# The second mixer's modulation blocks moved behind its projections, eight loads to a PSUM bank, and the output weights' low parts on VectorE

## The chip, the cores and the metric

The kernel runs on one core of a Trainium2 chip, in one launch. The metric is device time in microseconds (us): 2055.61 us, the median of 3 runs of the kernel before (2055.24 to 2056.08). About 4 us (0.2%) is what a comparison of this kernel can tell from no change.

## The reference, cut to what matters

Two transformer layers on 512 latent and 256 context tokens of width 1024. Both layers are scaled and shifted by rows that come out of a conditioning vector; layer 1 (odd) has differential attention, and each layer ends in a mixture of 32 experts.

```python
mod = jax.nn.silu(c) @ w_mod[l] + b_mod[l]          # (6 * 1024) values: six rows
sh1, sc1, gt1, sh2, sc2, gt2 = jnp.split(mod[:, None, :], 6, axis=-1)
h_lat = modulate(x, norm_mix[l], sh1, sc1)          # before the mixer
o_lat, o_ctx = mixer_c(h_lat, h_ctx, ...)           # projections, attention, @ w_out
x = x + gt1 * o_lat                                 # row 2
tokens = modulate(x, norm_ffn[l], sh2, sc2)         # rows 3 and 4
f = hier_moe(tokens, w_group[l], ...)               # router, then experts
x = x + gt2 * f                                     # row 5
```

The row products for layer 1 are a matrix of 1024 x 6144; rows 0 and 1 are made in the first mixer. Rows 2 to 5 (two blocks of 2048 columns, each in 8 loads of 128 x 2048 floats, 1 MB) are made in the second mixer, and they are what moves here.

## The kernel before, in words

Layer 1 runs in four stages, one after another: the second mixer (`mixer_c`), the output projection with the router (`out_proj`), the sorting of tokens by expert, and the experts (`moe`), whose weights stream from HBM.

**The mixer.** It works in 8 groups (heads). A group's projection (L261 to L263, three float32r products per piece, into the one bank of pool `ctp`, tag "pp") gives q, k and v for 6 token tiles; then 4 units, one per 128 latent tokens, make scores (L596 to L604), a maximum on VectorE (L1914), two exponentials on ScalarE (L1918), a combination on VectorE (L1931), transposes on TensorE (L618), their copies (L622) and the product with v (L633). The projection of group g+1 is laid among the units of group g; the last group's four units come after all projections.

**The order.** `Sched` is a list planner: each piece has an engine, an assumed duration, what it depends on, which buffers it takes and gives, and a position `pos`; among ready pieces of an engine, the lowest `pos` goes first. That fixes the program order of TensorE (PE), VectorE (DVE), ScalarE (ACT) and GpSimd (POOL), each of which runs strictly in its order. SyncE (SP) issues nearly all DMAs; its order follows from the rest, and it too goes in order: a DMA whose buffer is not free holds up all behind it.

**The modulation blocks.** `mod_later` loads a block's 8 tiles (L376) into the ring of four 1 MB buffers `wr`, which the projections' weights (L1738), the output weights (L1047) and the first expert weights (L1249) use as well. Each tile is multiplied by the silu columns (L381: 4 products of 128x512 in float32, which the trace shows as 8 records). Two tiles are summed in one bank of the pool that the transposes use (tag "pt", two banks), then added to a row buffer in `oo` by DVE (L475). After the 8 tiles the row goes to `modrow` in DRAM (L497); the second block is first multiplied with the norm's gain (L491). `first` and `end` spread the tiles over positions CM0 to CM1; CMW is how many tiles may be loaded ahead.

**The output weights.** `prepare_out` loads 4 MB of `w_out_c` and splits each half tile into a float32r high part on ACT (L322) and a low part (L325), the latter on POOL in layer 1. It begins when the projections and the rotary embedding (POOL, L550 to L566) are done, since its tiles take their memory; so do the router's weights (L1030 to L1033).

**`out_proj`.** Per token tile: transposes (L1105), their high and low parts (L1112, L1119), 48 products (`pop`, L261 to L263), the gate row `bc2` (L1159), the residual (L1162) and the router's logits (L1217). `fold_router` folds rows 3 and 4 into the router's weights: it loads them from `modrow` as columns (L1264, tile `mrows`, in two DMAs), transposes them on PE (L1269) and goes on with L1272, L1276 and L1281. Row 4 is in the second block. L503 spreads rows over 128 partitions, L1093 loads the residual.

```python
ld = S.op("DMA", 2.95, lambda k=k, load=load: load(k), [mms[-LA]], take=("wr", "mw"))
a = S.op("DMA", 0.6, load, pos=-9.0)                      # fold_router: mrows <- modrow
a = S.op("PE", 0.11, flip, [a], take=("pl",), pos=1.0)    # L1269
```

Of the kernel before, what the change touches and what calls it, by code (L numbers as in the profile page):

```python
# [20 lines left out]
KD = 8  # L21
# [59 lines left out]
CPREP = 3.79  # L81
CPACK = 0.8
CP0 = -37.415
CMW = 1
CM0 = 1.0
CM1 = 28.601
DPE = .217
DDVE = 0.15
DACT = .119
# [146 lines left out]
class Backbone:  # L236
# [197 lines left out]
        return self.mod_columns(0, lambda: st["row"], [a], psp, tag)  # L434


    def mod_later(self, jobs, rows_tile, nf, silp, psp, tag, first, end, after):
        nc, S = self.nc, self.S
        total, n, out = KD * len(jobs), 0, {}
        ready = S.op("POOL", 0.5, lambda: self.mod_sil(silp), [after], pos=first)  # L440
        mms = [ready] * LA
        for l, g in jobs:
            st = {}

            def rows(l=l, g=g, st=st):
                st["row"] = rows_tile()
                if (l, g) == (1, 0):
                    return
                nc.gpsimd.memset(st["row"], 0.0)
                if g == 2:  # L450
                    nc.gpsimd.memset(nf, 0.0)

            def biases(l=l, g=g, st=st):
                if (l, g) == (1, 0):
                    return
                for j in range(4):
                    b = 512 * (4 * g + j)
                    nc.sync.dma_start(st["row"][32 * j:32 * j + 2], self.i["b_mod"][l, b:b + 512].partition_broadcast(2))
                    if g == 2 and j < 2:
                        nc.sync.dma_start(nf[32 * j:32 * j + 2], self.i["norm_ffn"][l, 512 * j:512 * j + 512].partition_broadcast(2))  # L460

            def load(k, l=l, g=g, st=st):
                st[k] = self.mod_load(l, g, k)

            def mm(k, st=st):
                if k % 2 == 0:
                    st["ps"] = psp.tile([128, 512], F32, tag=tag, name="pmod")
                self.mod_mm(st["ps"], silp, st[k], k, k % 2 == 0, k % 2 == 1)

            def add(k, l=l, g=g, st=st):  # L470
                r = st["row"]
                if k == 1 and (l, g) == (1, 0):
                    nc.vector.tensor_copy(r, st["ps"])
                else:
                    nc.vector.tensor_tensor(r, st["ps"], r, op=OP.add)  # L475

            S.pos = first + (end - first) * n / total
            a = S.op("POOL", 0.4, rows, [ready], take=("mrow",))
            a = S.op("DMA", 0.3, biases, [a])
            for k in range(KD):  # L480
                S.pos = first + (end - first) * n / total
                n += 1
                ld = S.op("DMA", 2.95, lambda k=k, load=load: load(k), [mms[-LA]], take=("wr", "mw"))
                mms.append(S.op("PE", 1.0, lambda k=k, mm=mm: mm(k), [ld, mms[-1]], take=() if k % 2 else ("pt",), give=("wr", "mw")))
                if k % 2:
                    a = S.op("DVE", 0.62, lambda k=k, add=add: add(k), [mms[-1], a], give=("pt",))
            if (l, g) == (1, 0):
                out[l, g] = self.mod_columns(l, lambda st=st: st["row"], [a], psp, tag, ("mrow",))
                continue
            if g == 2:  # L490
                a = S.op("DVE", 0.62, lambda st=st: nc.vector.scalar_tensor_tensor(  # L491
                    st["row"][0:64], st["row"][0:64], 1.0, nf[0:64], op0=OP.add, op1=OP.mult), [a])

            def store(l=l, g=g, st=st):
                for j in range(4):
                    b = 512 * (4 * g + j)
                    nc.sync.dma_start(self.modrow[l][:, b:b + 512], st["row"][32 * j:32 * j + 2])  # L497

            out[l, g] = S.op("DMA", 0.3, store, [a], give=("mrow",))
        return out  # L500
# [510 lines left out]
    def prepare_out(self, l, wout, pos, after):  # L1011

        nc, S, i = self.nc, self.S, self.i
        self.pre, self.wo, parts = ExitStack(), [], {}
        pool = lambda n, b, **k: self.pre.enter_context(self.tc.tile_pool(name=n, bufs=b, **k))
        self.pool_out = ExitStack()

        def room():
            rp = pool("route", 1)
            t = lambda n, sh, d=F32: rp.tile(sh, d, name="r" + n)  # L1020
            self.rt = {
                "idx": t("idx", [128, NST], I32), "sw": t("sw", [128, 2, NST]), "ps": t("ps", [CAP, 2, NE]),
                "ord": t("ord", [1, NE], I32), "idx2": t("idx2", [128, NE], I32), "sw2": t("sw2", [128, 2, NE]),
                "idxb": t("idxb", [CAP, 8], I32), "swb": t("swb", [CAP, 2, 8]), "base": t("base", [128, NE]), "nb": t("nb", [NE, 2]), "ad": t("ad", [128, 2 * NT], I32),
                "pay": t("pay", [128, NT, 2, 2]), "tb": t("tb", [1, 3 * NOVB], I32), "oh": t("oh", [128, NT, 2, NE]),
                "w": t("w", [128, NT, 2]), "cum": t("cum", [128, NT + 1, NE]), "rank": t("rank", [128, NT, 2]),
                "ids": t("ids", [128, NT]), "wrt": t("wrt", [128, KD, 36]), "brt": t("brt", [128, 36]),
            }
            wrt, brt = self.rt["wrt"], self.rt["brt"]
            nc.sync.dma_start(wrt[:, :, 0:4], i["w_group"][l].rearrange("(k p) n -> p k n", k=KD))  # L1030
            nc.sync.dma_start(wrt[:, :, 4:36], i["w_expert"][l].rearrange("(k p) n -> p k n", k=KD))
            nc.sync.dma_start(brt[:, 0:4], i["b_group"][l].partition_broadcast(128))
            nc.sync.dma_start(brt[:, 4:36], i["b_expert"][l].partition_broadcast(128))  # L1033
            self.stay = pool("wmoe", NMOE)
            rest = self.pool_out.enter_context(self.tc.tile_pool(name="opw", bufs=KD - NMOE))
            for k in range(KD):
                w = (self.stay if k < NMOE else rest).tile([128, 2, 1024], F32R, tag="wr", name="wo")
                self.wo.append((w[:, 0], w[:, 1]))

        S.pos = pos  # L1040
        start = S.op("-", 0.0, room, after)
        for q in range(4):
            S.pos = pos + 2 * q

            def load(q=q):
                w = parts[q] = self.wtile().rearrange("p (k f) -> p k f", k=2)
                nc.sync.dma_start(w, wout[q * 256:(q + 1) * 256].rearrange("(k p) f -> p k f", p=128))  # L1047

            ld = S.op("DMA", 2.95, load, [start], take=("wr",))
            for k in range(2):  # L1050
                self.split_ops(lambda q=q, k=k: (*self.wo[2 * q + k], parts[q][:, k]), 1024, [ld], give=("wr",) if k else (),
                               low_on="POOL" if l else "DVE")


    def out_proj(self, l, oo, first, gain=None):
# [746 lines left out]
    def mixer_c(self, oo):  # L1802
        nc, tc, i = self.nc, self.tc, self.i
        S = self.S = Sched((DPE, DDVE, DACT, DPOOL), (EPE, EDVE, EACT, EPOOL), wr=NW, pt=2, s=2, po=1, pp=1, p0=2, p1=2, pts=2, qdup=1, qhl=2, rt=1, rt1=1, hss=2, khl=1,
                           grp=2, vv=3, whl=5, mrow=2, mw=CMW)
        keep, st = ExitStack(), ExitStack()
# [3 lines left out]
        pss, psm = right("cts", 2, space=PSUM), right("ctm", 2, space=PSUM)  # L1810
        pso, psp = right("cto", 1, space=PSUM), right("ctp", 1, space=PSUM)
# [23 lines left out]
        ld = S.op("DMA", 8.0, lambda: None)  # L1835

        sd = [S.op("DMA", 1.5, lambda t=t: nc.sync.dma_start(oo[:, t], self.source(1, t)), [ld]) for t in range(NT)]
        ld = S.op("DMA", 1.0, loads, sd)
# [7 lines left out]
        hdone, spare = {}, []  # L1846
# [23 lines left out]
        a = S.op("POOL", 0.5, lam_dots, [ld], pos=-20.0)  # L1870
        a = S.op("DVE", 0.2, lambda: nc.vector.tensor_reduce(ls, lp[:, 0::2], axis=AX.X, op=OP.add), [a], pos=-20.0)
        a = S.op("ACT", 0.1, lambda: nc.scalar.activation(ls, ls, AF.Exp), [a], pos=-20.0)
# [4 lines left out]
        end = self.in_proj(0, c, CP0, 0.0, [tables])  # L1877
        c.hdone = lambda t, q: []
        ropes = end
        for g in range(7):  # L1880
# [6 lines left out]
        room = [oo[:, 4 + m // 2, 512 * (m % 2):512 * (m % 2) + 512] for m in range(4)]  # L1887
        rows = iter(room[0:2])
        self.mod_later([(1, 1), (1, 2)], lambda: next(rows), room[2], room[3][:, 0:256].rearrange("p (k f) -> p k f", k=KD),
                       psm, "pt", CM0, CM1, S.op("-", 0.0, lambda: None, spare))  # L1890
        prev = dict.fromkeys(("s", "t", "v"))
        packed, squares = {}, {t: [] for t in range(4)}
        for j, (g, t) in enumerate(units):
# [163 lines left out]
```

## Time and profile before

| what | value |
|---|---|
| median of 3 runs | 2055.61 us |
| the profiled execution | 2057.26 us, its span 2055.5 us |
| PE busy | 1803.5 us (88%) |
| DVE, ACT, POOL busy | 984.2, 547.7, 316.7 us |
| DMA | 533.11 MB, 259 GB/s over the span |
| the second mixer, about | 1042 to 1456 us |
| `out_proj` of layer 1, about | 1456 to 1511 us |

How to read it: times are from the span's start. The stage in question lies between two stretches in which the DMA engines are full (the experts of layer 0 until about 1020 us, those of layer 1 from about 1533 us). In the mixer itself the DMA engines carry little, and PE is the busy one until the last projection; after it comes a stretch of some 50 us in which no engine is full. "Idle before" in a row is the time that the engine stood still before it, with the engine that released it.

### The profile page before, as it was taken

What the parts mean: (1) busy time and instruction counts of PE and PEld (TensorE: products, weight loads), DVE (VectorE), ACT (ScalarE), POOL (GpSimd) and SP (SyncE); (2) the same over time, 40 slices, a digit from 0 to 9 for tenths busy, and PEclk for the clock granted to TensorE, in tenths of its full rate; (3) what the DMA queues carried; (4) which work ended last, traced back from release to release, by engine and by line L of the source; (5) the groups of instructions that cost most, each with busy time, mean ns of one, the idle gap of its engine ahead of it and who ended that gap; (6) DMA issues with size and microseconds to landing.
All of it is one profiled execution on the core that took longest, in us unless ns stands there. A gap on an engine that the chain in (4) does not pass through costs nothing. (4 is left out here: it accounts for less than half of the span.)

```text
span 2055.5 us, 26431 instructions
## 1 busy us (share of the span) xinstructions
PE 1803.5 (88%) x9506; PEld 1063.1 (52%) x9506; DVE 984.2 (48%) x2572; ACT 547.7 (27%) x1259; POOL 316.7 (15%) x345
## 2 busy tenths in 40 slices
PE   4999988896999989989939999996869997898896
PEld 2798776684333332323328888885753332332232
DVE  4698778586223222222257878777781211111111
ACT  4564566221000000000054554554310000000000
POOL 2000000002022111111012222224121211111111
PEclk8999999997999999999969999998979999999999
DMA  8502314437999999999932223231459999999996
GB/s 348 186 28 88 124 45 164 154 134 249 369 376 393 406 405 401 397 391 405 375 114 73 73 98 119 73 124 44 175 210 353 356 401 410 414 403 413 412 410 259
DMA packets 97160, 533.11 MB, mean 259 GB/s; under 512 B 21938, under 2 KB 22306, under 8 KB 41728
## 3 DMA queue, kind: packets, MB, share of 16 engines
q1 hardware_dynamic: 82592, 510.32, 63.0%
q0 software_dynamic: 14432, 21.05, 4.3%
q8 instruction: 77, 1.26, 0.3%
q14 instruction: 59, 0.48, 0.1%
HBM read 518.24 MB, written 29.03 MB: 266 GB/s over the span
## 5 line engine op out<-in xcount | busy, mean ns | idle before, releaser
L1633 PE MATMUL h<-wr,x 128*64 128x512 f32 x1584 | 402.9, 612 | 62.5 <-DMA wr<-in_w_dram 62.4
L1633 PEld LDWEIGHTS h<-wr,x 128*64 128x64 f32 x1584 | 116.4, 139 | 280.9 <-issue 169.3
L1608 DVE COPY x<-trx 128x512 f32<-128x512 f32 (+1 forms) x69 | 44.1, 648 | 418.9 <-PE trx L1603 418.8
L1631 PE MATMUL h<-wr,x 128*96 128x512 f32 x416 | 203.7, 645 | 18.7 <-DMA wr<-in_w_dram 18.4
L1657 ACT ACTIVATE sl<-h 64x512 f32<-64x512 f32 (+1 forms) x64 | 37.9, 592 | 666.3 <-PE h L1633 468.0
L1692 PE MATMUL py<-wr,gt 128*64 128x512 f32 x816 | 188.5, 596 | 2.9 <-DMA wr<-in_w_dram 1.7
L1662 DVE TENSOR_TENSOR gp<-sl,h 64x512 f32<-64x512 f32 (+1 forms) x64 | 67.7, 1058 | 227.0 <-ACT sl L1657 142.3
L1631 PEld LDWEIGHTS h<-wr,x 128*96 128x96 f32 x416 | 71.2, 177 | 136.2 <-issue 117.9
L261 PE MATMUL pp<-wh,chh 128*128 128x384 f32 (+1 forms) x384 | 133.1, 347 | 5.6 <-ACT vv L687 3.7
L263 PE MATMUL pp<-wh,chl 128*128 128x384 f32 (+1 forms) x384 | 124.4, 324 | 0.9 <-DVE chl L325 0.9
L262 PE MATMUL pp<-wl,chh 128*128 128x384 f32 (+1 forms) x384 | 124.3, 324 | 0.0
L618 PE MATMUL ptp<-cst,p 128*128 128x128 f32 x592 | 97.0, 285 | 25.0 <-DVE p L1931 12.2
L1692 PEld LDWEIGHTS py<-wr,gt 128*64 128x64 f32 x816 | 57.1, 137 | 114.1 <-issue 99.2
L1520 POOL DMA_INDIRECT xg<-h2d,ridx x51 | 53.8, 1054 | 296.3 <-PE trx L1603 262.7
L618 PEld LDWEIGHTS ptp<-cst,p 128*128 128x128 f32 x592 | 70.1, 144 | 44.4 <-issue 18.3
L1690 PE MATMUL py<-wr,gt 128*96 128x512 f32 x208 | 92.2, 596 | 0.0
L1672 ACT COPY gt<-trg 128x256 f32<-128x256 f32 (+1 forms) x55 | 21.7, 394 | 239.4 <-PE trg L1668 239.4
L1535 DVE SCALAR_TENSOR_TENSOR y<-py,rsw,g 128x512 f32<-128x512 f32 x51 | 38.3, 751 | 97.1 <-PE py L1692 95.4
L261 PEld LDWEIGHTS pp<-wh,chh 128*128 128x128 f32 x384 | 74.2, 193 | 16.9 <-ACT vv L687 7.9
L941 ACT ACTIVATE p<-s,nbias,r 128x256 f32<-128x256 f32 (+3 forms) x96 | 76.6, 801 | 18.1 <-DVE nbias L935 8.0
L1527 POOL DMA_INDIRECT out_dram<-y,ridx x29 | 45.6, 1574 | 229.3 <-DVE y L1535 205.9
L622 ACT COPY pts<-ptp 128x384 f32<-128x384 f32 (+2 forms) x116 | 56.0, 488 | 76.0 <-PE ptp L618 75.3
(350 smaller groups left out, 3355.1 us busy)
## 6 DMA issues: line engine op xcount, KB each, us to landing
wr<-in_w_dram SPq DMA_DIRECT2D x378, 1024.0 KB
wr<-in_w_mod_dram SPq DMA_DIRECT2D x48, 1024.0 KB
wr<-in_wc_dram SPq DMA_DIRECT2D x16, 768.0 KB
wr<-in_wab_dram SPq DMA_DIRECT2D x8, 768.0 KB
oo<-in_w_dram SPq DMA_DIRECT2D x6, 1024.0 KB
h2d<-h2p SPq DMA_DIRECT2D x10, 512.0 KB
bc<-modrow SPq DMA_DIRECT2D x9, 512.0 KB
wr<-in_w_out_ab_dram SPq DMA_DIRECT2D x4, 1024.0 KB
```

The costliest lines, as they stand in the source:

```text
L261: mm(ps, xh, wh, start=start, stop=False)
L262: mm(ps, xh, wl, start=False, stop=False)
L263: mm(ps, xl, wh, start=False, stop=stop)
L618: nc.tensor.transpose(st[g][:, b], st["p"][:, (g + b) * 128:(g + b + 1) * 128], self.id)
L622: f(st["pts"][:, g:g + n], st[g][:, :n])
L941: nc.scalar.activation(p[:, a:b], st["s"][:, a:b], AF.Exp, bias=nb()[:, m:m + 1], scale=hr()[:, m:m + 1], accum_out=z["ssum"][:, h + m:h + ...
L1520: nc.gpsimd.indirect_dma_start(out=dst, out_offset=None, in_=src if big else halves(src), in_offset=bass.IndirectOffsetOnAxis(ap=idx, axis=0),
L1631: mm(x["h"][m][:CAP], x["k"](k), w, start=k == 0, stop=k == KD - 1)
L1633: mm(x["h"][0][CS * m:CS * m + CS], x["k"](k), w, start=k == 0, stop=k == KD - 1, tile_position=(0, CS * m), skip_group_check=True)
L1662: nc.vector.tensor_tensor(x["p"][:n].rearrange("t (k p) -> t p k", k=4), v(x["s"][:n]), v(x["h"][1][:n] if isb else x["h"][0][CS:128]), op ...
L1690: mm(x["y"][m][:CAP], x["gt"][:, k], w, start=k == 0, stop=k == 3)
L1692: mm(x["y"][0][CS * m:CS * m + CS], x["gt"][:, k, 0:CS], w, start=k == 0, stop=k == 3, tile_position=(0, CS * m), skip_group_check=True)
```

## The change

CMW goes from 1 to 2, CM0 from 1.0 to 26.9 and CM1 from 28.601 to 31.0: the 16 tiles take positions near the end of the 32 units instead of all along them. All 8 tiles of a block are summed in one bank (`run=KD`), which is now the projections' bank ("pp"), so that it is free only when the last projection has left it; DVE adds once per block instead of four times. The low parts of layer 1's output weights go from POOL to DVE. `mod_later` of the first mixer keeps `run=2`.

```diff
-CMW = 1
-CM0 = 1.0
-CM1 = 28.601
+CMW = 2
+CM0 = 26.9
+CM1 = 31.0
...
-    def mod_later(self, jobs, rows_tile, nf, silp, psp, tag, first, end, after):
+    def mod_later(self, jobs, rows_tile, nf, silp, psp, tag, first, end, after, run=2):
...
             def mm(k, st=st):
-                if k % 2 == 0:
+                if k % run == 0:
                     st["ps"] = psp.tile([128, 512], F32, tag=tag, name="pmod")
-                self.mod_mm(st["ps"], silp, st[k], k, k % 2 == 0, k % 2 == 1)
+                self.mod_mm(st["ps"], silp, st[k], k, k % run == 0, k % run == run - 1)
...
-                if k == 1 and (l, g) == (1, 0):
+                if k < run and (l, g) == (1, 0):
...
-                mms.append(S.op("PE", 1.0, lambda k=k, mm=mm: mm(k), [ld, mms[-1]], take=() if k % 2 else ("pt",), give=("wr", "mw")))
-                if k % 2:
-                    a = S.op("DVE", 0.62, lambda k=k, add=add: add(k), [mms[-1], a], give=("pt",))
+                mms.append(S.op("PE", 1.0, lambda k=k, mm=mm: mm(k), [ld, mms[-1]], take=() if k % run else (tag,), give=("wr", "mw")))
+                if k % run == run - 1:
+                    a = S.op("DVE", 0.62, lambda k=k, add=add: add(k), [mms[-1], a], give=(tag,))
...
-                               low_on="POOL" if l else "DVE")
+                               low_on="DVE")
...
-                       psm, "pt", CM0, CM1, S.op("-", 0.0, lambda: None, spare))
+                       psp, "pp", CM0, CM1, S.op("-", 0.0, lambda: None, spare), KD)
```

PE, before, where the mixer ends and `out_proj` begins (`po` is attention's last product, `ot` the first transposes of `out_proj`, `pop` its products, `pc` the router's rows):

```order
L618 MATMUL ptp<-cst,p 128x128 x6
L633 MATMUL po<-vv,pts 128x128 x6
L1105 MATMUL ot<-cst,oo 128x128 x8
L261 MATMUL pop<-wo,oh 128x512
L262 MATMUL pop<-wo,oh 128x512
L263 MATMUL pop<-wo,ol 128x512
L261 MATMUL pop<-wo,oh 128x512
L262 MATMUL pop<-wo,oh 128x512
L263 MATMUL pop<-wo,ol 128x512
L1269 MATMUL pc<-cst,mrows 128x16
```

PE, now, at the same place (`pmod` x4 is one tile of a modulation block):

```order
L633 MATMUL po<-vv,pts 128x128 x3
L1105 MATMUL ot<-cst,oo 128x128 x8
L633 MATMUL po<-vv,pts 128x128 x3
L381 MATMUL pmod<-wr,oo 32x512 x8
L261 MATMUL pop<-wo,oh 128x512
L262 MATMUL pop<-wo,oh 128x512
L263 MATMUL pop<-wo,ol 128x512
L261 MATMUL pop<-wo,oh 128x512
L262 MATMUL pop<-wo,oh 128x512
L263 MATMUL pop<-wo,ol 128x512
L381 MATMUL pmod<-wr,oo 32x512 x16
L1269 MATMUL pc<-cst,mrows 128x16
```

The first ten tiles stand among the last units, all behind the last projection; the last six stand behind attention's last product, four of them right ahead of the router's transposes.

SP, before, from the output weights to `out_proj` (the second `modrow` store and all 16 tiles of the blocks lie ahead of this):

```order
L1047 DMA wr<-in_w_out_c_dram 128x2x1024 x4
L497 DMA modrow_88<-oo 2x512 x4
L1030 DMA rwrt<-in_w_group_dram 128x8x4
L1031 DMA rwrt<-in_w_expert_dram 128x8x32
L1032 DMA rbrt<-in_b_group_dram 128x4
L1033 DMA rbrt<-in_b_expert_dram 128x32
L1249 DMA wr<-in_w_dram 128x2048 x4
L1264 DMA mrows<-modrow_88 8x128 x2
L503 DMA bc_12943<-modrow_88 128x1024
```

SP, now, from the last piece of the output weights (`bc_12931` is the gate row, `bc_12944` row 3):

```order
L1047 DMA wr<-in_w_out_c_dram 128x2x1024
L1264 DMA mrows<-modrow_88 8x128
L376 DMA wr<-in_w_mod_dram 128x2048
L503 DMA bc_12931<-modrow_88 128x1024
L376 DMA wr<-in_w_mod_dram 128x2048
L503 DMA bc_12944<-modrow_88 128x1024
L376 DMA wr<-in_w_mod_dram 128x2048
L1093 DMA xi<-xd 128x1024 x2
L376 DMA wr<-in_w_mod_dram 128x2048
L1249 DMA wr<-in_w_dram 128x2048 x6
L497 DMA modrow_88<-oo 2x512 x4
L1264 DMA mrows<-modrow_88 8x128
```

The two halves of `mrows` are apart now: the first stands ahead of the last four tiles, the second behind them, behind all six loads of expert weights and behind the second block's store.

DVE, now, among the last two units (`wo` is a low part of the output weights):

```order
L1931 SCALAR_TENSOR_TENSOR p<-p,cf 128x768
L325 TENSOR_TENSOR wo<-wr,wo 128x1024
L1943 TENSOR_SCALAR oo<-po,rz 128x128
L325 TENSOR_TENSOR wo<-wr,wo 128x1024
L1914 TENSOR_REDUCE nbias<-s 128x1 x2
L1924 TENSOR_TENSOR nbias<-nbias,r_11920 128x1
```

The eight low parts, which POOL had in one run behind its last rotary embedding, stand one or two at a time in DVE's order: four among the last units, four behind them.

## Rows read from the trace of the kernel before

**Rows 1.** Busy time by stage: the projections, then the last units.

```profile
core 0: us, PE busy (x) PEld busy (x) DVE busy (x) ACT busy (x) POOL busy (x), PEclk, DMA share, GB/s
1092.00:1404.00 312.00, 303.17 (x2055) 273.91 (x2053) 240.10 (x682) 163.43 (x404) 79.95 (x127) 1.00 0.27 92
1404.00:1457.00 53.00, 30.07 (x148) 25.23 (x147) 41.23 (x105) 24.31 (x52) 23.39 (x16) 0.74 0.26 83
```

**Rows 2.** Timeline, PE at one tile of a block: start us, us, engine, line.

```profile
1380.74 1.07 PE L381 MATMUL pmod<-wr,oo 128*32 128x512 f32 x8
1381.73 0.55 PE L618 MATMUL ptp<-cst,p 128*128 128x128 f32 x3
```

**Rows 3.** Timeline, PE from the last projection to the router's transposes.

```profile
1404.00 0.34 PE L263 MATMUL pp<-wh,chl 128*128 128x384 f32 x1
1404.17 0.40 PE L596 MATMUL s<-kt,qh 128*128 128x512 f32 x1
...
1452.56 2.93 PE L633 MATMUL po<-vv,pts 128*128 128x128 f32 x12
...
1459.07 0.23 PE L1269 MATMUL pc<-cst,mrows 16*128 16x16 f32 x1
```

**Rows 4.** Timeline, POOL's low parts of the output weights (first and last row).

```profile
1422.78 4.65 POOL L325 TENSOR_TENSOR wo<-wr,wo 128x1024 fp32r<-128x1024 f32 x2 [12.90 <-ACT wo L322]
...
1441.85 6.99 POOL L325 TENSOR_TENSOR wo<-wr,wo 128x1024 fp32r<-128x1024 f32 x3 [4.91 <-ACT wo L322]
```

**Rows 5.** Timeline, DVE then: three of seven stretched rows, and L1931 alone.

```profile
1424.25 0.89 DVE L1928 SCALAR_TENSOR_TENSOR cf<-rz,lam,ssum 128x1 f32<-128x1 f32 x1
...
1434.89 2.86 DVE L1931 SCALAR_TENSOR_TENSOR p<-p,cf 128x768 f32<-128x768 f32 x1
...
1446.59 2.26 DVE L293 TENSOR_TENSOR rsq<-rsy 128x8 f32<-128x8 f32 x1
...
1449.87 1.01 DVE L1931 SCALAR_TENSOR_TENSOR p<-p,cf 128x768 f32<-128x768 f32 x1
```

**Rows 6.** Waits of PE, 1404 to 1457: us in total, times, longest.

```profile
PE ptp L618 <- DVE p L1931: 11.9, 3, 5.1
```

**Rows 7.** Waits of DVE, 1404 to 1457.

```profile
DVE nbias L1914 <- PE s L604: 6.6, 7, 2.0
DVE oo L1943 <- PE po L633: 3.0, 3, 1.1
```

**Rows 8.** Groups of DVE by shape over the span: busy us, mean ns.

```profile
L325 DVE TENSOR_TENSOR wo<-wr,wo 128x1024 fp32r<-128x1024 f32 x8 | 9.7, 1219 | 0.0
...
L475 DVE TENSOR_TENSOR oo<-pmod,oo 128x512 f32<-128x512 f32 x8 | 5.5, 685 | 0.8 <-PE pmod L381 0.7
...
L491 DVE SCALAR_TENSOR_TENSOR oo<-oo 64x512 f32<-64x512 f32 x1 | 0.7, 684 | 0.0
```

**Rows 9.** Timeline, SP's issues of layer 1.

```profile
1409.09 0.40 SPq L1030 DMA_DIRECT2D rwrt<-in_w_group_dram  x1
...
1456.40 0.64 SPq L1264 DMA_DIRECT2D mrows<-modrow  x2
```

**Rows 10.** Waits of SP, 1404 to 1480.

```profile
SPq L1264 <- ACT csq L1947: 7.1, 1, 7.1
```

**Rows 11.** The DMA rate while weights stream (last column), experts of layer 0.

```profile
850.00:900.00 50.00, 45.44 (x186) 14.83 (x180) 15.09 (x21) 2.52 (x5) 9.45 (x7) 0.97 1.02 404
```

**Rows 12.** Timeline, SP in layer 0: two 1 MB loads, then four small ones.

```profile
380.56 0.80 SPq L1249 DMA_DIRECT2D wr<-in_w_dram  x2
381.75 1.50 SPq L1264 DMA_DIRECT2D mrows<-modrow  x4
```

**Rows 13.** The first microsecond of DMA after that issue.

```profile
381.00:382.00 1.00, 0.00 (x0) 0.00 (x0) 0.42 (x1) 0.51 (x2) 0.00 (x0) 1.00 0.74 115
```

**Rows 14.** Timeline, PE in layer 0, which waits for the small ones.

```profile
388.75 0.28 PE L1269 MATMUL pc<-cst,mrows 32*128 32x32 f32 x1 [4.40 <-DMA mrows<-modrow]
...
389.56 0.63 PE L262 MATMUL pop<-wo,oh 128*128 128x512 f32 x1
```

## The prediction

> **What bounds the kernel now.** I first read the busy time by stage, to see which engine each stage hangs on, then the timeline of PE, DVE, POOL and SP around the stage that changes, then who waited for whom there.
>
> While projections run (1092 to 1404 us) PE is busy 303.2 of 312 us at the full granted clock, 2.4 GHz; DVE is at 77%, and the DMA engines move 92 GB/s [rows 1]. What leaves PE's order there shortens the stage by about its own length. After the last projection the picture changes: PE is busy 30.1 of 53 us, its mean granted clock is 0.74, which mixes stretches at 2.4 and at 1.2 GHz, and no engine is full [rows 1]. That tail is one chain: scores, maximum, exponential, combination, transposes, product. PE waits 11.9 us in it for the combination alone [rows 6], and DVE waits for PE in turn [rows 7]. All below is counted from the end of the projections, 1404.17 [rows 3], as p.
>
> In the tail before, attention's last product begins at p+48.4 (1452.56) and the router's transposes L1269 run at p+54.9 (1459.07) [rows 3], without a wait. Between them SP issues `mrows` at p+52.2, released by ScalarE's last square (csq), whose memory it takes [rows 9, 10]. From L1269 on, `out_proj` is dense on PE, so I take the time from L1269 to the end as unchanged: what shifts L1269 shifts the end.
>
> **The change part by part.**
>
> *Removed from the projections: 16 tiles on PE.* One tile takes 0.99 us of PE's order (1381.73 - 1380.74) [rows 2]. 16 x 0.99 = 15.8 us come off a stage that PE bounds. Upper bound: 15.8 + the stage's 8.8 us of idle PE = 24.6; lower bound 8, if half becomes waits for what DVE and ACT must still do. I take 15.8, since PE is 97% busy. Six of eight DVE adds of 0.69 us [rows 8] go too; DVE has 72 us free there, so nothing more.
>
> *POOL's low parts become DVE's.* POOL's last row ends at 1448.84 [rows 4], and a small DVE instruction, L293, ends with it at 1448.85 after 2.26 us; L1931 takes 2.86 us beside POOL's rows and 1.01 alone [rows 5]. Seven rows are stretched so; over what the same instructions take elsewhere in the tail that is 0.7 + 2.1 + 1.1 + 1.9 + 0.6 + 1.3 + 2.1 = 9.7 us. POOL's work goes, and these with it. In return DVE does 8 parts of 1.22 us [rows 8], 9.8 us. By order, four of them (4.9) and one add (0.7) lie ahead of attention's end, the other four behind it. One block tile stands between attention's product and the key transposes that the last group waits for: +1.0. The others among the units stand where PE waits anyway. So attention ends at p+(-9.7 + 4.9 + 0.7 + 1.0), 3.1 us earlier. Bounds: -9.7 (the new work lies all in the 9.6 us that DVE waits for PE [rows 7]) to +4 (the stretched rows lay beside a wait, and half of the new work adds to it). I stay with -3.1: PE's 11.9 us for the combination [rows 6] says that the stretched rows were on the chain.
>
> *Added to the tail: 14 of the 16 block loads.* Two tiles load early and the rest start when the last projections' buffers come free. SP's order is what counts. Right ahead of the last four tiles it has the first half of `mrows`, which must wait for the last csq as before [rows 10]: p+52.2 - 3.1 = p+49.1. Only then come tile, gate row, tile, row 3, tile, two residual tiles, tile, six expert loads; then the second block's store, and then the second half of `mrows`, which L1269 needs. 4 tiles, two rows spread to 0.5 MB each, two residual tiles of 0.5 MB and 6 MB of experts are 12 MB. At 404 GB/s [rows 11] that is 12 x 1.049 / 0.404 = 31.1 us. It begins about 0.4 us (the issue) and 0.9 us (issue to first packets, from 380.56 to the busy microsecond at 381 [rows 12, 13]) after p+49.1: p+50.4 to p+81.5.
>
> The buffers don't break this stream: each of the last loads waits for a tile's product three loads earlier, which PE does as soon as it lands. The store's own input is ready well before: the last tile lands after 6 of the 12 MB, p+66.0, then 1 us on PE, 0.69 and 0.68 on DVE [rows 8], p+68.4. But its packets stand behind those of the expert loads issued before it. Rows of layer 0 show that this is so: four `mrows` transfers issued until 383.25, behind two 1 MB loads, released PE at 388.75 after 4.40 us of idling [rows 12, 14], 5.5 us later, whereas those of layer 1, with nothing ahead, were there 2.4 us after their issue at most (1456.40 + 0.3 to 1459.07) [rows 3, 9]. 2 MB at 404 GB/s are 5.2 us, so the difference is the queue.
>
> The Trainium skill (DMA: Bandwidth & Descriptors, Queues, rings and completion order) says that each DMA engine takes descriptors in ring order, while completions of different transfers need not come in order. By ring order the store waits as in my sum; if the second half decided, the rival below with 2060 would come. Layer 0's 5.5 us agree with ring order.
>
> So the store lands about 1 us behind the stream, p+82.5, and `mrows` 2.4 us later: L1269 at p+84.9 instead of p+54.9, +30.0 us. Bounds: p+73.7, if small transfers don't wait behind loads (p+68.4 plus 2.4 for the store, 2.4 for `mrows`, and half a microsecond of issue), and p+90, if the 12 MB flow at 360 GB/s. On PE all of `out_proj`'s products but the first six stand behind L1269.
>
> *After the stall.* In layer 0 the granted clock has fallen in the wait, and a 128x512 product takes 0.63 us instead of 0.39 [rows 14]. Here PE will have idled 15 us. Some twelve products at 0.43 us apart instead of 0.24 make 2; before, PE came from a slow stretch too, so +1, bounds 0 and 3.
>
> **Sum.** -15.8 + 30.0 + 1.0 = +15.2, against the profiled execution, 2057.26 us (1.7 above the median of the timed runs; span 2055.5). Applied to the median: 2055.6 + 15.2 = 2070.8; I say 2070.
>
> **The rivals.**
> - *Small transfers overtake* (2060). Store and `mrows` don't wait behind expert loads: L1269 at p+73.7, +18.8 - 15.8 + 1.0 = +4. For it: they are a few KB. Against: layer 0's rows.
> - *The tail closes up* (2046), the one on the other side. The block loads and the last units run beside each other, all 9.7 us of stretched rows come off (6.6 more than in my sum), PE's 8.8 us of idling in the projections go as well, and store and `mrows` overtake: 73.7 - 6.6 - 54.9 - 15.8 - 8.8 = -12, with the clock's +1 and some of each left, -10. It decides for faster from the point where L1269 comes before p+70.7 (54.9 + 15.8). Against: even without any queue, 6 MB of loads come after csq, 15.6 us, so attention would have to end by about p+43.
> - *PE stops inside attention* (2076 or more). Ten tiles and three quarters of the output weights share four buffers among the last units; SP holds them behind L1030, which waits for the rotary embedding until p+4.9 [rows 9]. A tile's product that waits for its load holds up the scores behind it. Two loads that are 3 us late make +6. For it: a buffer comes free only when PE or DVE has passed what is in it. Against: PE passes those ten tiles in some 45 us, 4.5 each, and 1 MB needs 2.6 us at 404 GB/s.
> - *The tiles don't leave the projections*: excluded by PE's order.
>
> **How the numbers follow.** My sum (range 2063 to 2077): 0.62. Overtaking: 0.14, half of it within 0.2%. PE stops inside: 0.14. Tail closes up: 0.10, nearly all of it faster. 0.2% of 2055.6 is 4 us, about what a measurement can tell from no change. Slower: 0.62 + 0.14 + 0.07 = 0.83; same 0.08; faster 0.09. The range 2057 to 2079 leaves out the faster cases, a part of the same ones and the worst of the stops inside, together 0.2.
>
> **What would show it.** The projections' stage 15 to 17 us shorter and without L381; no stretched rows on DVE in the tail; attention's end at p+45 to p+50; DMA full at about 400 GB/s from there for some 30 us; PE standing before L1269 with `mrows` as releaser, 10 us or more, and L1269 at about p+85. The forecast is wrong if L1269 comes before p+74 (small transfers not queued, or loads earlier than I think), or if `out_proj` after L1269 takes another time than before.

## The result and the profile after

The changed kernel takes 2068.23 us (median of 4 runs, 2066.22 to 2070.24), the kernel before in the same comparison 2055.85 us: ratio 1.0059, 95% interval 1.0046 to 1.0071, which is 9.5 to 14.6 us slower. The prediction was 2070 us, 2057 to 2079, slower with 0.83. Its sign and its chain were right; its terms were off by up to 3 us each, in both directions, so that the errors partly cancel, and one of them for a reason that is worth the reading.

The profiled execution spans 2066.9 us (before 2055.5). First the busy time by stage, with the columns of [rows 1]: the projections, the tail up to attention's end, and the time from there to L1269.

```profile
1074.00:1386.00 312.00, 297.26 (x1993) 282.64 (x1992) 251.72 (x718) 170.96 (x420) 79.92 (x133) 0.99 0.11 38
1386.00:1432.00 46.00, 36.94 (x239) 22.53 (x242) 35.24 (x111) 23.85 (x52) 4.76 (x8) 0.89 0.75 272
1432.00:1467.00 35.00, 9.67 (x50) 1.75 (x42) 11.11 (x24) 3.26 (x4) 0.00 (x0) 0.60 0.92 368
```

Against [rows 1], the projections move 38 GB/s instead of 92: the block loads have left. The tail has them, at 272 GB/s, and PE's granted clock there is 0.89 instead of 0.74. The third line is new: 35 us in which PE works 9.7 and the DMA engines move 368 GB/s.

PE's timeline beside [rows 3]; the last column is the idle time ahead of a row and what ended it.

```profile
1385.82 0.34 PE L263 MATMUL pp<-wh,chl 128*128 128x384 f32 x1
1386.00 0.39 PE L596 MATMUL s<-kt,qh 128*128 128x512 f32 x1
...
1430.25 0.83 PE L633 MATMUL po<-vv,pts 128*128 128x128 f32 x6
...
1441.61 1.94 PE L381 MATMUL pmod<-wr,oo 128*32 128x512 f32 x8 [3.30 <-DMA wr<-in_w_mod_dram]
...
1450.41 1.94 PE L381 MATMUL pmod<-wr,oo 128*32 128x512 f32 x8 [3.10 <-DMA wr<-in_w_mod_dram]
...
1467.09 0.25 PE L1269 MATMUL pc<-cst,mrows 16*128 16x16 f32 x1 [14.75 <-DMA mrows<-modrow]
...
1474.06 1.09 PE L1105 MATMUL ot<-cst,oo 128*128 128x128 f32 x8
```

The projections end 18.2 us earlier (1386.00 for 1404.17), but L1269 comes 8.0 us later, at p+81.1 instead of p+54.9, after 14.75 us of standing for `mrows`. The same products between L1269 and the next L1105 then take 6.97 us, where they took 4.30 before (1459.07 to 1463.37). So L1105 is 10.7 us late, and the span in the end 11.4.

SP's timeline beside [rows 9], then its waits beside [rows 10].

```profile
1432.04 0.29 SPq L1264 DMA_DIRECT2D mrows<-modrow  x1
...
1438.37 0.33 SPq L376 DMA_DIRECT2D wr<-in_w_mod_dram  x1
1439.86 12.87 SPq L1249 DMA_DIRECT2D wr<-in_w_dram  x6
1453.13 2.46 SPq L497 DMA_DIRECT2D modrow<-oo  x4
1465.66 0.26 SPq L1264 DMA_DIRECT2D mrows<-modrow  x1
```

```profile
SPq L1264 <- DMA modrow<-oo: 10.0, 1, 10.0
...
SPq L1264 <- ACT csq L1947: 3.6, 1, 3.6
```

The last block load is issued at 1438.37, six expert loads of 1 MB from 1439.86, the store of 4 x 4 KB from 1453.13. SP then waits 10.0 us for that store before it may issue the second half of `mrows`. The DMA engines are full meanwhile (busy share and GB/s in the last two columns), and PE does nothing:

```profile
1456.00:1460.00 4.00, 0.00 (x0) 0.00 (x0) 0.00 (x0) 0.00 (x0) 0.00 (x0) 0.50 1.01 422
```

### The profile page after: what moved, and what is told of

It is laid out like the page before. It is cut to its first block, busy times and chain, and to the rows that moved or that the text cites. A ratio compares the mean times of both kernels' runs of the same rounds, so it can differ in the third digit from the quotient of the medians.

```text
span 2066.9 us, 26407 instructions
## 1 busy us (share of the span) xinstructions
PE 1802.1 (87%) x9506; PEld 1059.4 (51%) x9506; DVE 982.8 (48%) x2575; ACT 546.7 (26%) x1258; POOL 294.6 (14%) x337
## 5 line engine op out<-in xcount | busy, mean ns | idle before, releaser
L1631 PE MATMUL h<-wr,x 128*96 128x512 f32 x416 | 199.2, 633 | 17.1 <-DMA wr<-in_w_dram 16.9
L261 PE MATMUL pp<-wh,chh 128*128 128x384 f32 (+1 forms) x384 | 131.8, 343 | 6.6 <-ACT vv L687 4.6
L263 PE MATMUL pp<-wh,chl 128*128 128x384 f32 (+1 forms) x384 | 124.7, 325 | 0.9 <-DVE chl L325 0.9
L262 PE MATMUL pp<-wl,chh 128*128 128x384 f32 (+1 forms) x384 | 124.6, 324 | 0.0
L941 ACT ACTIVATE p<-s,nbias,r 128x256 f32<-128x256 f32 (+3 forms) x96 | 76.5, 800 | 18.1 <-DVE nbias L935 8.0
L261 PEld LDWEIGHTS pp<-wh,chh 128*128 128x128 f32 x384 | 74.6, 194 | 9.8 <-ACT vv L687 7.5
L1188 POOL TENSOR_TENSOR h2p<-xi,bc 128x512 f32<-128x512 f32 x10 | 16.2, 1617 | 443.5 <-DVE xi L1185 322.1
```

Of the source, the lines that this page charges most:

```text
L261: mm(ps, xh, wh, start=start, stop=False)
L262: mm(ps, xh, wl, start=False, stop=False)
L263: mm(ps, xl, wh, start=False, stop=stop)
L941: nc.scalar.activation(p[:, a:b], st["s"][:, a:b], AF.Exp, bias=nb()[:, m:m + 1], scale=hr()[:, m:m + 1], accum_out=z["ssum"][:, h + m:h + ...
L1631: mm(x["h"][m][:CAP], x["k"](k), w, start=k == 0, stop=k == KD - 1)
```

## The experiments

Every run is compared with the kernel before on the same chip; the changed kernel stands at 1.0059. Differences between two runs are taken from these ratios; with their intervals they are good to about 3 us. The stages ahead of p are the same in all kernels with the same tiles among the projections, yet p itself scatters (six kernels with the whole move: 1384.75 to 1388.59; four without: 1402.69 to 1406.13). The scatter lies ahead of the second mixer's first scores (L596, at 1116.87 before): from there to p kernels with the same tiles agree within 0.2 us. Why is open. So places are counted from p. "Routing's end" is L1394, the first of the last counts ahead of the experts. From there to the end of the span every one takes 521.8 to 524.3 us.

| kernel | ratio to before (95%) | p | L1269 | routing's end |
|---|---|---|---|---|
| before | 1 | 1404.17 | p+54.9 | p+129.5 |
| changed | 1.0059 (1.0046 to 1.0071) | 1386.00 | p+81.1 | p+158.4 |
| e1_low | 0.9971 (0.9962 to 0.9980) | 1406.13 | p+49.9 | p+124.5 |
| e1_low2 | 0.9966 (0.9954 to 0.9978) | 1403.61 | p+49.5 | p+124.1 |
| e2_mods | 1.0074 (1.0060 to 1.0089) | 1386.77 | p+85.2 | p+162.0 |
| e3_hold | 1.0005 (0.9995 to 1.0015) | 1388.24 | p+72.5 | p+149.4 |
| e4_poolq | 1.0039 (1.0026 to 1.0052) | 1386.59 | p+79.4 | p+155.8 |
| e5_fold | 0.9996 (0.9987 to 1.0004) | 1388.59 | p+81.2 | p+147.8 |
| e8_holdfold | 0.9946 (0.9933 to 0.9959) | 1384.75 | p+71.5 | p+138.0 |
| e11_half | 0.9919 (0.9906 to 0.9932) | 1392.48 | p+53.1 | p+127.7 |
| e12_halfhold | 0.9952 (0.9939 to 0.9965) | 1394.16 | p+52.2 | p+129.1 |
| e14_fill | 0.9956 (0.9942 to 0.9969) | 1402.69 | p+48.5 | p+123.1 |

**e1_low: the low parts alone.**

```diff
-                               low_on="POOL" if l else "DVE")
+                               low_on="DVE")
```

> The kernel before with one line changed: VectorE takes the eight low parts of the output weights, the modulation blocks stay among the projections. Theory A (step 2 of the prediction: the rows stretched beside POOL are on the tail's chain): no row of L1931 over 1.5 us in the tail; attention's last product, at p+48.4 in the kernel before, 4.8 us earlier (9.7 us of stretch away, four low parts of 1.22 us added), time 2051 us. Rival B (the tail of the changed kernel is shorter because the block tiles fill PE's waits and keep its granted clock up, 0.89 instead of 0.76; VectorE's side is not what limits): the stretched rows go, but attention's end moves by less than 2 us and the clock of the tail stays near 0.76: 2054 to 2057 us.

Measured: 2051.65 us, ratio 0.9971, 6.0 us faster than before; L1269 at p+49.9, 5.0 us earlier, now in this row of PE's timeline:

```profile
1455.99 0.23 PE L1269 MATMUL pc<-cst,mrows 16*128 16x16 f32 x1
```

No L1931 is longer than 1.444 us (before 2.856). The rows stretched beside POOL were on the chain, as theory A says; the same kernel run again (e1_low2) has L1269 5.4 us earlier. But that theory A's sum fits to 0.2 us is luck. It added four low parts ahead of attention's end; in this trace all eight stand there, 9.8 us of VectorE, the last of them just ahead of the last combination:

```profile
1444.96 1.22 DVE L325 TENSOR_TENSOR wo<-wr,wo 128x1024 fp32r<-128x1024 f32 x1
1447.22 1.01 DVE L1931 SCALAR_TENSOR_TENSOR p<-p,cf 128x768 f32<-128x768 f32 x1
```

By the theory's own prices that would have left no gain (-9.7 + 9.8). So the exchange is shown, and not what a stretched row or an added part costs. This half of the change is a gain by itself.

**e2_mods: the move alone.** The line of e1_low put back in the changed kernel.

> The changed kernel with POOL doing the low parts of the second mixer's output weights again; only the modulation blocks are moved. Theory A: the rows of VectorE beside POOL's are stretched again and lie on the chain, so attention's last product comes 4.8 us later than in the changed kernel (p+44.3 to p+49), and since the loads of the last tiles stand behind it, L1269 and the end too: 2073 us. Rival B (tiles among the units keep the clock up, whoever makes the low parts): clock of the tail near 0.89 and attention's end within 2 us of the changed kernel's: 2067 to 2070 us.

Measured: ratio 1.0074, 15.2 us slower than before; L1269 at p+85.2, 4.1 later than in the changed kernel. SP's and PE's timelines:

```profile
1437.77 0.29 SPq L1264 DMA_DIRECT2D mrows<-modrow  x1
```

```profile
1471.94 0.26 PE L1269 MATMUL pc<-cst,mrows 16*128 16x16 f32 x1 [9.74 <-DMA mrows<-modrow]
```

The first half of `mrows` goes out at p+51.0, in the changed kernel at p+46.0: again 5.0 us for the low parts, here with four of the eight ahead of attention's end: theory A. But before it was p+52.2. With POOL doing the low parts in both, the tiles among the units made the tail 1.2 us shorter, where I had added 1.7.

**e3_hold: the expert loads out of the way.**

```diff
-            for q, (m, e, half) in enumerate(self.early_order()):
-                S.op("DMA", 2.95, lambda m=m, e=e, half=half: self.early_load(l, m, e, half), pos=12.0 + 3 * q)
             folded = self.fold_router(l, nt, big, ps1)
+            for q, (m, e, half) in enumerate(self.early_order()):
+                S.op("DMA", 2.95, lambda m=m, e=e, half=half: self.early_load(l, m, e, half), [S.op("DVE", 0.06, lambda m=m, e=e, half=half: self.early_hold(m, e, half), [self.held], pos=1.0)] if l else (), pos=12.0 + 3 * q)
...
+def early_hold(self, m, e, half):
+    t = self.early[m, e, half] = self.wtile()
+    self.nc.vector.tensor_copy(t[:, 0:1], self.ab0)
```

> The changed kernel with the six early expert loads held back: each waits for a one-column write by VectorE behind L1272, so SP issues them after the second block's store and its mrows half. PE's order is the same. Theory A (step 3: store and mrows stand in the queue behind 6 MB of expert loads): the last tile's product still ends at p+66, the store lands some 2.5 us after its issue and mrows 2.4 us after that, L1269 at p+74 instead of p+81.1; time 7 to 9 us less than the changed kernel, 2060 us. Rival B (the store and mrows take that long by themselves, whatever is in the queue): L1269 stays at p+81, time 2068 us. Rival C (the expert loads, 20 us later, are then late for the first expert): L1269 early but the end at 2068 us or later.

Measured: ratio 1.0005, 11.1 us less than the changed kernel (7.8 from p to the end by the traces). SP and PE:

```profile
1457.01 1.24 SPq L497 DMA_DIRECT2D modrow<-oo  x4
1459.26 0.26 SPq L1264 DMA_DIRECT2D mrows<-modrow  x1
```

```profile
1460.75 0.25 PE L1269 MATMUL pc<-cst,mrows 16*128 16x16 f32 x1 [4.53 <-DMA mrows<-modrow]
```

With nothing ahead of it the store has landed 2.25 us after its first issue, and `mrows` is at PE 1.5 us after its own. L1269 comes 8.6 us earlier, routing 9.0. Theory A is shown: of the 14.75 us that PE stood ahead of L1269, 10.2 were the expert loads in the queue (1.6 of them are lost again, since the last tile comes later). Rival C is not seen.

**e4_poolq: the same transfers, another queue.**

```diff
-                    nc.sync.dma_start(self.modrow[l][:, b:b + 512], st["row"][32 * j:32 * j + 2])
+                    (nc.gpsimd if (l, g) == (1, 2) else nc.sync).dma_start(self.modrow[l][:, b:b + 512], st["row"][32 * j:32 * j + 2])
...
-                    nc.sync.dma_start(rows[8 * (n * m + v):8 * (n * m + v) + 8],
+                    (nc.gpsimd if l and m == 0 else nc.sync).dma_start(rows[8 * (n * m + v):8 * (n * m + v) + 8],
```

> The changed kernel with the second block's store and the mrows half behind it issued on POOL's queue instead of SP's; PE, DVE, ACT and the rest of SP's order are the same, and the six expert loads stay in SP's queue. Theory A (they wait because of their place in SP's queue): they go past the expert loads, L1269 at p+74 to p+76 (POOL makes its descriptors itself, so up to 1 us more for each of the two), time 2060 to 2063 us. Rival B (they wait because the sixteen DMA engines are full, whichever queue they are in): L1269 at p+81 or later, 2068 us or more.

Measured: ratio 1.0039, L1269 at p+79.4, 1.7 us earlier. POOL's timeline, then the landing times of POOL's queue (last number, us) among the DMA issues:

```profile
1454.66 2.23 POOL L497 DMA_DIRECT2D modrow<-oo  x4 [62.34 <-DVE oo L491]
1460.95 0.52 POOL L1264 DMA_DIRECT2D mrows<-modrow  x1 [4.07 <-DMA wr<-in_w_dram]
```

```profile
modrow<-oo POOLq DMA_DIRECT2D x4, 4.0 KB, 5.0
mrows<-modrow POOLq DMA_DIRECT2D x1, 4.0 KB, 4.9
```

```profile
1465.95 0.25 PE L1269 MATMUL pc<-cst,mrows 16*128 16x16 f32 x1 [13.07 <-DMA mrows<-modrow]
```

Neither theory. A 4 KB transfer in another queue neither passes the expert loads nor waits them out: 5 us, against 10 behind them in one queue and about 2 with nothing ahead. (POOL's 4.07 us are put down to an expert load that came last; what the second transfer needs is the store.) But here both transfers meet full engines, one after the other, where in SP's queue only the store did; so half the wait twice saves little. The Trainium skill (DMA: Bandwidth & Descriptors, Queues, rings and completion order) says that an engine takes turns between the queues it has work for, a packet at a time; the 5 us agree in kind.

**e5_fold: PE's order instead of the queue.** In `fold_router` each `pos=1.0` from the transposes on becomes a later place.

```diff
-        a = S.op("PE", 0.11, flip, [a], take=("pl",), pos=1.0)
+        a = S.op("PE", 0.11, flip, [a], take=("pl",), pos=8.0 if l else 1.0)
```

> The changed kernel with the router's fold (L1269 to L1295 of the second layer) given a later place in out_proj, 8.0 instead of 1.0; by the order 42 products of out_proj's first two token tiles come ahead of block tiles 13 to 16, and L1269 behind those. The queue is as in the changed kernel. Theory A (what the queue costs is PE standing in its order before L1269): the 42 products, 0.24 us apart, go into the time in which PE waited for the last loads and for mrows, so L1269 stays near p+81 but 10 us of out_proj lie ahead of it, and no slow products follow: 2056 to 2058 us. Rival B (the routing behind L1269 is the chain that ends out_proj, PE's products are not): 2064 to 2068 us.

Measured: 2056.74 us, ratio 0.9996, 13.0 us less than the changed kernel. L1269 is as late as before the edit and still waits:

```profile
1469.80 0.28 PE L1269 MATMUL pc<-cst,mrows 16*128 16x16 f32 x1 [11.89 <-DMA mrows<-modrow]
```

but from it to routing's end PE needs 66.6 us instead of 77.3. Theory A: the late `mrows` cost what it did because products that don't need it stood behind it. Only its last clause fails: six products behind L1269 are slow here too (0.63 us). What the later place would do in the kernel before, where L1269 does not wait, was not run.

**e8_holdfold: both.** The diffs of e3_hold and e5_fold together.

> Both edits at once: the six expert loads held behind mrows and the router's fold at place 8.0. Theory A (one stall, two causes, and what is left of it with the loads held, 4.5 us before L1269 and 11 us before tiles 13 to 16, is filled by products): 6 to 10 us less than with the loads held alone, 2048 to 2052 us. Rival B (with the store and mrows no longer queued, L1269 comes as early as PE can use it, and the later fold only delays the routing): within 2 us of the loads held alone, 2057 to 2060 us.

Measured: 2047.06 us, ratio 0.9946, 12.1 us less than e3_hold, somewhat more than theory A's 6 to 10. Routing ends at p+138.0, 20.4 us earlier than in the changed kernel; the two edits alone gave 9.0 and 10.6. They add up. PE's waits from attention's end to L1269 show how:

```profile
PE pc L1269 <- DMA mrows<-modrow: 4.5, 1, 4.5
PE pmod L381 <- DMA wr<-in_w_mod_dram: 1.4, 2, 0.9
```

In e3_hold the same two are 4.5 and 11.0 us. Holding the loads shortens the wait for `mrows`; the products that the later fold lets ahead fill the waits for the last tiles, and what is left of the wait for `mrows` stays.

**e11_half: half the move.**

```diff
-        self.mod_later([(1, 1), (1, 2)], lambda: next(rows), room[2], room[3][:, 0:256].rearrange("p (k f) -> p k f", k=KD),
-                       psp, "pp", CM0, CM1, S.op("-", 0.0, lambda: None, spare), KD)
+        free = S.op("-", 0.0, lambda: None, spare)
+        [self.mod_later([(1, g)], lambda: next(rows), room[2], room[3][:, 0:256].rearrange("p (k f) -> p k f", k=KD), pool, tag, a, b, free, run) for g, pool, tag, a, b, run in ((1, psm, "pt", 1.0, 14.8, 2), (2, psp, "pp", 26.9, 29.0, KD))]
```

> The changed kernel with only half of the move: block (1, 1) stays among the projections in banks of two tiles as before, block (1, 2) comes behind them; VectorE does the low parts. Theory A (the tail has room for 8 MB of block loads among its units, what was too much was the 16 beside the residual tiles and the experts): projections 8.5 to 9 us shorter, the tail as in the changed kernel up to attention's end (p+45), and L1269 at p+50 to p+53 with no more than 3 us of waiting: 2042 to 2047 us. Rival B (any block behind the projections makes mrows wait for a store behind the expert loads): L1269 at p+60 or later, 2051 us or more.

Measured: 2042.91 us, ratio 0.9919 (0.9906 to 0.9932), the fastest of all: 16.7 us less than before (14.7 by the medians). SP's and PE's timelines:

```profile
1433.47 0.52 SPq L497 DMA_DIRECT2D modrow<-oo  x2
1436.11 0.36 SPq L1249 DMA_DIRECT2D wr<-in_w_dram  x1
1442.74 0.60 SPq L1264 DMA_DIRECT2D mrows<-modrow  x2
```

```profile
1445.54 0.23 PE L1269 MATMUL pc<-cst,mrows 16*128 16x16 f32 x1
```

The last store is out 9 us ahead of the issue of `mrows`, which waits for the last csq as in the kernel before, and L1269 comes without a wait at p+53.1. That is theory A, but two of its terms missed, against each other. From the first scores to p the kernel takes 11.3 us less than before, where I had 8.5 to 9. And the tail is not that of the changed kernel: `mrows` is issued at p+50.3, not p+46.0, after PE has stood for VectorE ahead of the last transposes:

```profile
1437.91 0.85 PE L618 MATMUL ptp<-cst,p 128*128 128x128 f32 x6 [3.96 <-DVE rsq L294]
```

VectorE has three low parts and the block's add and gain between the last scores and the last combination there. So the tail is 3.4 to 3.8 us longer than without the move (e1_low, e1_low2); whether the loads or only VectorE's order make it so was not tried. Beside e1_low, which has none of the move, half of it is worth 10.7 us, and all of it costs 18.1; by the traces, from the first scores to the end, 9.4 and 15.1.

**e12_halfhold: half the move, expert loads held.** e11_half with the diff of e3_hold.

> The half move with the six expert loads held behind mrows. Theory A (the three expert loads that SP issues ahead of mrows in the half move do not delay it, since it waits for the last csq anyway): L1269 as in the half move, and the same time or, if the experts come late, up to 2 us more: 2042 to 2049 us. Rival B (they do delay it): 2 to 6 us less than the half move.

Measured: 2048.39 us, ratio 0.9952, 6.8 us more than e11_half by the ratios, 5.5 by the medians, 2.4 from p to the end by the traces. L1269 is 0.9 us earlier, so the loads did not delay it (not rival B). But routing's end is 1.4 later. PE and VectorE show why:

```profile
1452.61 0.41 PE L1285 MATMUL pb<-sh,pick 1*128 1x36 f32 x2 [2.20 <-DVE sh L1292]
```

```profile
1452.25 0.21 DVE L2061 COPY wr<-mcols 128x1 f32<-128x1 f32 x2
1452.38 0.17 DVE L1292 COPY sh<-ps 1x36 f32<-1x36 f32 x1
```

L1292 stands behind attention's last rows and two of the holding writes (L2061). That explains 2 us; whether the rest is the scatter ahead of p stays open.

**e14_fill: work that nobody needs.** Why had the tiles made the tail shorter? In e1_low's kernel each of the last five units gets two groups of four products on constants:

```diff
-            unit(u)
+            unit(u); self.fill(psp, j, 27, 2, prev)
...
+        for i in range(4):
+            self.nc.tensor.matmul(st["ps"][32 * i:32 * i + 32], self.id[:, 0:32], self.cst[:, 0:512], start=k == 0,
+                                  stop=k == n - 1, tile_position=(0, 32 * i), skip_group_check=True)
...
+    last = prev["s"]
```

> The kernel before with the low parts on VectorE, and besides ten groups of four products among the last five units of attention, of the block tiles' form (32x512) but on constants that lie in SBUF and into a bank that nobody reads: 10 us of work on PE that nothing needs, with no loads. Theory A (the block tiles among the units cost nothing there, since PE stands waiting and slow anyway, and its clock rises with them): the granted clock of the tail 0.85 or more instead of 0.81, attention's end within 1 us of that without the groups (last product's start p+45), and time within 2 us of it, 2049 to 2052 us. Rival B (each tile stands in PE's order ahead of scores that are waited for): attention's end 3 to 6 us later, time 2053 to 2057 us.

> The kernel before with the low parts on VectorE once more, beside the run with the added products: 2050 to 2052 us by either theory; the attention's last product near p+45, the clock of the tail near 0.81.

Measured: 2049.72 us (0.9956) with the products, 2051.67 us (0.9966) without. From p to the end of attention, with the columns of [rows 1], e14_fill and then e1_low2:

```profile
1402.69:1447.00 44.31, 33.88 (x219) 22.24 (x218) 36.51 (x105) 23.78 (x48) 4.78 (x8) 0.92 0.31 99
```

```profile
1403.61:1448.80 45.19, 27.41 (x139) 22.25 (x138) 36.74 (x105) 23.68 (x48) 4.75 (x8) 0.77 0.31 97
```

Theory A, and a little beyond it: 9.6 us of products in 80 instructions, and PE is busy only 6.5 us more, because its granted clock is 0.92 instead of 0.77 (0.81 in e1_low, the same kernel) and what must be done is done faster. L1269 is 1.0 us earlier. In time the two can't be told apart.

## Why the prediction was right, step by step

- *Projections, -15.8.* Measured 18.2 in the profiles, part of it p's scatter. Without the scatter, from the first scores to p, before and now:

```profile
1116.87:1404.17 287.30, 280.01 (x1903) 254.07 (x1903) 223.74 (x640) 153.56 (x380) 70.25 (x111) 1.00 0.26 87
1115.89:1386.00 270.11, 263.28 (x1792) 251.13 (x1792) 223.51 (x638) 150.92 (x374) 67.59 (x111) 1.00 0.11 38
```

  17.2 us for the 14 tiles that lie in this stretch, 1.23 each and not 0.99 (all six kernels with the whole move take 270.1 to 270.3, all four without 287.3 to 287.4). The price of a tile was too small because it was only the tile's own start-to-start distance; the instructions on both sides of it are slower too:

```profile
1179.68 0.34 PE L262 MATMUL pp<-wl,chh 128*128 128x384 f32 x1
1179.85 0.34 PE L263 MATMUL pp<-wh,chl 128*128 128x384 f32 x1
1180.12 1.06 PE L381 MATMUL pmod<-wr,oo 128*32 128x512 f32 x8
1181.12 0.45 PE L261 MATMUL pp<-wh,chh 128*128 128x384 f32 x1
1181.40 0.34 PE L262 MATMUL pp<-wl,chh 128*128 128x384 f32 x1
```

  L262 to L263 takes 0.17 us, but L263 to the tile 0.27 and L261 behind it 0.28.
- *Attention's end, -3.1.* Measured 6.2 (first half of `mrows` at p+46.0 for p+52.2). For the low parts I had -9.7 + 4.9 = -4.8, and the exchange gave 5.0 to 5.7 by the issue of `mrows`. That this fits is luck: it is nearly the same with four parts ahead of attention's end (e2_mods against the changed kernel, 5.0) and with all eight (e1_low 5.4, e1_low2 5.7), so neither the 9.7 nor the 1.22 a part is shown. The step that failed is the +1.7 for a tile and an add; it was -0.5 to -1.2 (the kernels with the tiles against those without, with the low parts on the same engine), since I had priced a tile by its own length and not by what it does to a waiting PE's clock. e14_fill, whose products have no loads, agrees: its tail is 0.9 us shorter; each of these is one profile. The waits of PE that I read as the chain [rows 6] shrank accordingly (1386 to 1432):

```profile
PE ptp L618 <- DVE p L1931: 3.0, 2, 1.9
```

- *Queue, 12 MB behind the first half of `mrows`.* From that issue to L1269 I had 35.8 us (p+49.1 to p+84.9), measured 35.1 (p+46.0 to p+81.1). The rate over the stream was close to my 404 GB/s, below it at first and above it later:

```profile
1433.30:1465.00 31.70, 8.37 (x38) 1.43 (x36) 9.80 (x22) 2.00 (x2) 0.00 (x0) 0.59 0.99 397
```

  The store had landed 33.6 us after that issue where I had 33.4, and `mrows` then took 1.4 us to L1269 instead of 2.4. The store waits for the expert loads (10.0 us for SP; e3_hold). This is the term that decides the sign.
- *The clock after the stall, +1.* Measured 2.7: 6.97 us from L1269 to L1105 against 4.30. I had thought that PE came from a slow stretch before too; in the kernel before it did not lose anything there (4.30, as in e1_low). Mis-sized, within its bounds.
- *Sum.* -18.2 + 26.2 (L1269 from p+54.9 to p+81.1) + 2.7 = +10.7 where I had +15.2. The span grew by 11.4 and the medians differ by 12.4, so that the time behind L1269 is unchanged, as I took it, but for the clock and less than 1 us.
- *Rivals.* Small transfers do not overtake in SP's queue. PE does not stop inside attention: its waits for block loads are all behind attention's end (9.7 us at four tiles). The tail did close up, by 6.2 us, but would have had to end by p+43.

## What to carry to other kernels

Work moved off a full engine into a latency-bound tail is cheap there as long as its loads fit: price the tail's bytes first, and look at what small dependent transfer is issued behind the bulk. An instruction that waits for such a transfer belongs behind everything on its engine that doesn't need it. And half of a move can be worth more than the whole: the whole cost some 15 to 18 us, half gained 9 to 11.

## What the runs showed of the hardware that I had not expected

- 9.6 us of products that nobody reads, put into a stretch of 45.2 us where PE is busy for 27.4, made it no longer (44.3 us): the granted clock rose from 0.77 (0.81 in the other run of that kernel) to 0.92. The Trainium skill (TensorE: Matmul & The Clock Gate, Part 1: The HAM clock gate) says that the clock follows how busy PE has lately been; the two rows agree.
- A 4 KB transfer, or four issued together, takes about 2 us on quiet DMA engines (e3_hold), 5 when the six expert loads are under way in another queue (e4_poolq), and 10 behind them in its own (the changed kernel).
- The clock's price did not grow with the last wait: from L1269 to L1105 it is 6.48 us in e3_hold (1460.75 to 1467.23), after 4.53 us of standing, 6.52 in e2_mods after 9.74, 6.12 in e4_poolq after 13.07, and 6.97 in the changed kernel, after 14.75, against 4.30 without. In all of them PE had been waiting for loads, tile by tile, since attention's end; in the changed kernel the granted clock is at its lower level, 1.2 GHz (0.50), from 1440 on, 12 us before the last wait begins:

```profile
1440.00:1467.00 27.00, 5.80 (x24) 0.60 (x24) 3.48 (x4) 0.00 (x0) 0.00 (x0) 0.50 0.92 382
```
